# Moving operands laid at multiples of 64 bytes, block products reordered, and block sums made in place, in a two-layer diffusion trunk

## The chip, the cores and the metric

The kernel runs on one core of one Trainium2 chip. The metric is the device time of one execution in microseconds; the figure for a kernel is the median of its runs. A profile of one further execution gives the engines' instructions: PE (TensorE matmuls), PEld (its weight loads), DVE (VectorE), ACT (ScalarE), POOL (GpSimd) and SP (SyncE, which issues the DMAs).

## What is computed

Two layers over 1,024 latent tokens and 256 context tokens of width 1,024. Layer 0 mixes tokens by neighbourhood attention, layer 1 by sliding-window attention with grouped queries. Both end with a gated ConvFFN, which is where most of the change lies:

```python
def conv_ffn(h, w_up, conv_w, conv_b, w_down):
    t = h.shape[1]
    u = h @ w_up
    u_p = jnp.pad(u, ((0, 0), (CONV_W // 2, CONV_W // 2), (0, 0)))
    u = sum(u_p[:, tap:tap + t] * conv_w[tap] for tap in range(CONV_W)) + conv_b
    a, g = jnp.split(u, 2, axis=-1)
    return (a * jax.nn.silu(g)) @ w_down

for i in range(DEPTH):
    ...
    x = x + gt1 * (o @ w_out)
    ...
    h = modulate(rmsnorm(x, g_ffn[i]), sh2, sc2)
    x = x + gt2 * conv_ffn(h, ffn_w_up[i], ffn_conv_w[i], ffn_conv_b[i], ffn_w_down[i])
```

In layer 0 the context tokens go through the same ConvFFN; in layer 1 only the latents do.

## The kernel before

**Precision.** Every product is made of three: an operand is split into a high part (`hi`, a rounded copy made by ACT) and the rest (`lo`, the difference, made by DVE or POOL), and PE adds hi·hi, lo·hi and hi·lo into one bank. So one product step of the program is three matmuls: weights `whi`, `whi`, `wlo` against moving `hi`, `lo`, `hi`. In the FFN the weights are the stationary side, 128×128 at a time, and the activations the moving side: the moving operand is a row of 512 floats in each partition (256 for context tokens), of `b1hi`, `t12hi`, `t34h`, `b22hi` and their low parts, or of `ghi` and `glo` in the down projection.

**Up projection by blocks.** `ffn(l, ...)` runs the up projection of 1,024 tokens as a 2×2×2 block product with seven block multiplications instead of eight. The tokens are two halves (c = 0, 1), the 1,024 input features two halves (k below 4, and from 4), and the output pair of features (the `a` half and the `g` half of the gated product) the two column blocks. On the activation side this needs four sums of blocks, made once per layer: `t1` = X12−X11, `t2` = X22+shift−t1, `t3` = X22+dsh−X12, `t4` = X21+shift−t2 (X are the normalized and scaled tiles; `shift` and `dsh` bring in the adaLN shift). Each sum is then split into hi and lo: `t1`, `t2` in `t12hi`/`t12lo`, `t3`, `t4` in `t34h`/`t34l`. For each of the 22 feature tiles (`ft`) the weights need four sums too (`s`, from the two raw tiles `wraw`), and then seven products of 4 k-steps × 3 matmuls run on PE: 84 matmuls of 512 columns. `PROD` gives their order. The products go to four banks: `ua` (b11, then b21 on top), `ub` (t2), `uc` (t3, then t4), `ud` (t1, then b22). Between the two products of a bank ACT or DVE reads the bank's first state: ACT copies `ua` to the scratch `p1`, DVE adds `ub` to it, and so on, until the four quarters `c` of the tile's result are there. Then three convolution taps (`u`), SiLU, the product a·silu(g) on POOL, and a DMA of the tile to `g_dram`.

**Down projection.** `dn` reads `g_dram` back (`graw`), splits it into `ghi`, `glo`, splits the weights, and runs 22 × 8 × 3 matmuls of 512 columns for each token half of each layer: 2,112 in all. Each matmul reads `ghi` or `glo` as the moving operand.

**Context FFN.** In layer 0, `plan_ctx` runs the context's FFN (`uc`←`h2c`, 48 matmuls of 256 columns per feature tile, and `dnc`←`g`, 24) just ahead of the up projection; the block sums are made in its shadow. In layer 1 no context FFN stands there, so the normalization, the block sums and the first feature tile follow each other directly.

**Order of work.** A planner (`Sched`) is given operations with an engine, a duration, what they read and write, a key (a due time) and buffers to acquire and release; it plays them through and issues them in the order in which its model started them. On the chip each engine takes its own instructions strictly in that order, and waits on semaphores for the others. A change of keys or of dependencies therefore moves instructions on all engines. Since one wrapper issues every instruction, all of them carry line L79 in the profile, and one goes by tile names.

**Where tiles lie.** Tiles are allocated one behind another in a partition. In the built program of the kernel before, every tile starts at a multiple of 32 bytes. Of 16,148 matmuls, 4,712 have a moving operand that starts 32 bytes past a multiple of 64, the others start at a multiple of 64. The 4,712 are: all 2,112 of `dn` (512 columns), all 1,056 `uc`←`t34h`/`t34l` (512), all 528 of `dnc` (256), 592 `pv`←`pthi` and 304 `pv`←`ptlo` of attention (256), 96 `pv`←`pthi` (128) and 24 small ones of the norm. All other 512-column products of the FFN (`b1`, `t12`, `b22`) and of the output projection (`oacc`) start at a multiple of 64. The odd 32 bytes come from small tiles in front: `dsh`, 4 floats, in the FFN, and the attention scratch `S`, 644 floats, of which several buffers lie ahead of `pthi` and `ptlo`.

Of the kernel before, what the change touches and what calls it, by code (L numbers as in the profile page):

```python
# [241 lines left out]
def trunk_kernel(ctx, tc, xperm, xseq, cc, wmod, bmod, gnorm, na_wqkv, na_gq, na_gk, na_bias, na_wo,  # L242
# [334 lines left out]
    def plan_su(sc, key, I, units, groups, psa, wk, reads, write, n_add):  # L577
# [28 lines left out]
        for k in range(2):  # L606
# [98 lines left out]
    def plan_norm(sc, l, psa, wk, sums, x, hl, key):  # L705
# [46 lines left out]
        def dg(e):  # L752
            B["dg"] = wk.tile([P, 644], F32, tag="S", name="S", bufs=SBUFS)
# [11 lines left out]
        def bs(e):  # L765
            B["bc"] = wk.tile([P, 644], F32, tag="S", name="S", bufs=SBUFS)
# [472 lines left out]
    def ffn(l, opj, xt1, todo):  # L1239
# [117 lines left out]
        def plan_xload(c, key):  # L1357
            X[c] = Parts([None] * 4, 2)
            uses = 6 if c == 0 else 0
            for j in range(4):  # L1360
                def load(e, j=j):
# [4 lines left out]
                      acq=[("x", ("xt", c, j), uses or (4 if j < 2 else 8))])  # L1366
# [206 lines left out]
        sc.op("dve", 0.07, lambda e: dve.tensor_tensor(out=dsh, in0=shift[:, 4:8], in1=shift[:, 0:4], op=ALU.subtract),  # L1573
              writes=[("dsh",)], key=-50)
        rx = lambda c, k: [("xt", c, k // 2)] if X[c] is not xt1 or not last else []
        kb = 46.0 * n_todo
        for k in range(KT):
# [3 lines left out]
                      key + 0.5, rx(0, k))  # L1581
        for j in range(4):
            key = kb + (30.0 if not last else 2.0) * j
            for k in (j, j + 4):
                plan_t(1, 512, Nm[1], k, xap(1), xtok(1), scale, key)
            J = {}
            a, b = ("tr", j, "a"), ("tr", j, "b")
            x11, x21, x12, x22 = [lambda c=c, k=k: X[c][:, k, :] for c, k in ((0, j), (0, j + 4), (1, j), (1, j + 4))]
            k11, k21, k12, k22 = ("x", 0, j), ("x", 0, j + 4), ("x", 1, j), ("x", 1, j + 4)
            sh = shift[:, j + 4:j + 5]  # L1590
# [6 lines left out]
            def stt(out, in0, s, in1):  # L1597
                return lambda e: dve.scalar_tensor_tensor(out=out(), in0=in0(), scalar=s, in1=in1(), op0=ALU.add, op1=ALU.subtract)
            sc.op("dve", t_dve(512) + 0.06, stt(lambda J=J: J["a"][:, 512:], x22, sh, lambda J=J: J["a"][:, :512]),
                  reads=[k22, a + (1,)], writes=[a + (2,)], key=key, rel=rx(1, j + 4))  # L1600

            def t3(e, J=J, x12=x12, x22=x22, j=j):
                J["b"] = sr_tile("t34")
                dve.scalar_tensor_tensor(out=J["b"][:, :512], in0=x22(), scalar=dsh[:, j:j + 1], in1=x12(), op0=ALU.add,
                                         op1=ALU.subtract)
            sc.op("dve", t_dve(512) + 0.06, t3, reads=[k22, k12, ("dsh",)], writes=[b + (1,)], key=key, acq=[("sr", b, 2)],
                  rel=rx(1, j) + rx(1, j + 4))
            sc.op("dve", t_dve(512) + 0.06, stt(lambda J=J: J["b"][:, 512:], x21, sh, lambda J=J: J["a"][:, 512:]),
                  reads=[k21, a + (2,)], writes=[b + (2,)], key=key, rel=rx(0, j + 4))
            hcs = [("hc", k, "l") for k in range(KT)] if not last else []  # L1610
            for r, s, hi, lo, nm in ((a, "a", lambda j=j: t12h()[:, 2 * j:2 * j + 2, :].rearrange("p k t -> p (k t)"),
                                      lambda j=j: t12l(j).rearrange("p k t -> p (k t)"), "t12"),
                                     (b, "b", lambda j=j: t34_(0)[:, j, :], lambda j=j: t34_(1)[:, j, :], "t34")):
                sc.op("act", t_act(1024), lambda e, s=s, J=J, hi=hi: act.activation(hi(), J[s], AF.Copy), reads=[r + (1,), r + (2,)] + hcs,
                      writes=[(nm, j, "h")], key=key, rel=[r])
                sc.op(*LO[1024], lambda e, s=s, J=J, hi=hi, lo=lo: sub(e, lo(), J[s], hi().bitcast(F32)),
                      reads=[(nm, j, "h"), b + (2,)], writes=[(nm, j, "l")], key=key, rel=[r])

            hold = [("hcu",)] if not last else [("t34", i, "h") for i in range(4)] + [("b1", k, "l") for k in range(KT)]
            B22 = (512, j + 4, xap(1), xtok(1), shift, lambda j=j: b2h()[:, j, :], lambda j=j: b2l()[:, j, :], ("b2", j), key + 1,  # L1620
                   rx(1, j + 4))
            B["plan", j] = (hold, B22)
        for j in range(4):
            hold, a = B["plan", j]
            sc.op("x", 0.0, lambda e: None, reads=hold, writes=[("hcfree", j)], key=-100)
            n, k, x, xk, s, hi, lo, tok, key, rel = a
            sc.op("act", t_act(n), lambda e, hi=hi, x=x, k=k, s=s: act.activation(hi(), x(k), AF.Identity, bias=s[:, k:k + 1]),
                  reads=[xk(k), ("hcfree", j)], writes=[tok + ("h",)], key=key, rel=rel)
            sc.op("dve", t_dve(n) + 0.06, lambda e, hi=hi, lo=lo, x=x, k=k, s=s: dve.scalar_tensor_tensor(
                out=lo(), in0=x(k), scalar=s[:, k:k + 1], in1=hi().bitcast(F32), op0=ALU.add, op1=ALU.subtract),  # L1630
                reads=[xk(k), tok + ("h",)], writes=[tok + ("l",)], key=key, rel=rel)
# [7 lines left out]
            t1=(lambda j: (t12h()[:, 2 * j, :], t12l(j)[:, 0, :]), lambda j: ("t12", j)),  # L1639
            t2=(lambda j: (t12h()[:, 2 * j + 1, :], t12l(j)[:, 1, :]), lambda j: ("t12", j)),  # L1640
            t3=(lambda j: (t34_(0)[:, j, :512], t34_(1)[:, j, :512]), lambda j: ("t34", j)),
            t4=(lambda j: (t34_(0)[:, j, 512:], t34_(1)[:, j, 512:]), lambda j: ("t34", j)))
        PROD = (("a", 0, 0, "b11", True), ("b", 1, 0, "t2", True), ("a", 0, 512, "b21", False), ("c", 1, 512, "t3", True),
                ("d", 2, 0, "t1", True), ("c", 3, 0, "t4", False), ("d", 2, 512, "b22", False))

        def plan_up(ft):
            key = KU + 19.2 * ft
            pk = key - 24
            R, S, W = {}, {}, {}
            T = lambda *a: ("up", ft) + a  # L1650
# [15 lines left out]
            def plan_w(p, src, n, reads, rel, uses):  # L1666
                sc.op("act", t_act(n), whi(p, src, n), reads=reads, writes=[T("w", p, "h")], key=pk + p, acq=[("w", T("w", p), uses)],
                      rel=rel)
                sc.op(*LO[n], wlo(p, src, n), reads=reads + [T("w", p, "h")], writes=[T("w", p, "l")], key=pk + p, rel=rel)

            def s_op(e, t, c, make, a, b, op):
                if make:
# [5 lines left out]
                  reads=[rg] + ([("t34", 3, "h"), ("t34", 3, "l")] if ft else []),  # L1678
# [7 lines left out]
                  reads=[ra, T("s", 1), T("s", 2)], writes=[T("s", 4)], key=pk, rel=[ra])  # L1686
            plan_w(1, lambda: S[2], 1024, [T("s", 3), T("s", 4)], [T("s23")], 8)
            plan_w(2, lambda: S[1], 1024, [T("s", 4)], [T("s14")], 8)
# [4 lines left out]
            def plan_p(i):  # L1693
                d, p, col, b, first = PROD[i]
                ap, tok = BP[b]
                for j in range(4):
                    def mm(e, j=j):
# [4 lines left out]
                        for m, (w, x) in enumerate(((0, hi), (0, lo), (1, hi))):  # L1702
# [4 lines left out]
                          writes=[T("u", d)], key=key + 2.72 * i, acq=[("b", T("u", d), {"a": 2, "b": 1, "c": 2, "d": 2}[d])]  # L1707
                          if first and j == 0 else (), rel=[T("w", p)])
# [12 lines left out]
            sc.op("act", t_actp(512), p1, reads=[ua], writes=[st], key=key - 30, acq=[("sr", st, 3)], rel=[ua])  # L1721
# [5 lines left out]
            s_ = lambda: C["s"][:, :512]  # L1727
            tdp = t_dve(512) + 0.02
            sc.op("dve", tdp, pu(s_, "b", s_), reads=[ub], writes=[st], key=key - 30, rel=[ub])
# [565 lines left out]
```

## Time and profile before

| what | value |
|---|---|
| runs of the kernel | 3,006.07, 3,006.94, 3,008.57 us; median 3,006.94 |
| the profiled execution's own time | 3,010.63 us |
| its span from first to last instruction | 3,008.6 us |
| mean granted TensorE clock | 0.986 |
| matmuls in the profile | 16,608 |

The page gives busy time and instruction count of each engine, then the span in 40 slices with the busy share in tenths. A matmul's own duration in the profile overlaps the next one's, so what a matmul costs on a busy PE is the distance from its start to the start of the next; this text calls that the pitch. Starts are read from the timeline, whose rows are: start in us, duration in us, engine, line, operation, out<-in, shapes, count, and in brackets the idle time before it and what ended that.

### The profile page before, as it was taken

To read this page: it belongs to the slowest core of one execution; us is meant where nothing else is said; L and a number is where in the kernel's file an instruction comes from. 1 tells how busy PE (TensorE), PEld (TensorE's weight loads), DVE (VectorE), ACT (ScalarE), POOL (GpSimd) and SP (SyncE) were. 2 spreads that over 40 slices of the span, in tenths; PEclk is the share of its full clock that TensorE was granted. 3 is DMA by queue.
4 is the path that set the end of the run, shared out by engine and by line. 5 is a ranking of instruction groups with operands and counts; after the bars stand their busy time and mean duration, and the time that the engine had idled before them with its cause. 6 is when DMAs were issued, how large, how long until landed. Compare 5 with 4: busy or idle time off the path is not lost. (4 is left out here: it accounts for less than half of the span.)

```text
span 3008.6 us, 46247 instructions
## 1 busy us (share of the span) xinstructions
PE 2906.3 (97%) x16608; PEld 2509.3 (83%) x16608; DVE 2317.4 (77%) x4958; ACT 1638.7 (54%) x3168; POOL 740.4 (25%) x826
## 2 busy tenths in 40 slices
PE   6999999998999999999999999999998899999999
PEld 4999999998889977777788788988877688888887
DVE  7888888888787778787855659999987988887333
ACT  4777777777455534343433548887863444444222
POOL 2221222222110023232211025445421433332000
PEclk9999999999999999999999989999999999999999
DMA  6222222225645443434464630000133122224553
GB/s 234 61 84 81 84 83 62 75 76 157 215 156 188 154 164 122 144 123 137 141 224 147 219 122 29 14 31 14 68 125 118 69 79 77 85 84 168 170 170 102
DMA packets 126165, 349.88 MB, mean 116 GB/s; under 512 B 19440, under 2 KB 29168, under 8 KB 124528
## 3 DMA queue, kind: packets, MB, share of 16 engines
q1 hardware_dynamic: 125936, 346.94, 34.7%
q8 instruction: 131, 2.15, 0.3%
q14 instruction: 98, 0.80, 0.1%
HBM read 297.21 MB, written 49.68 MB: 115 GB/s over the span
## 5 line engine op out<-in xcount | busy, mean ns | idle before, releaser
L79 ACT ACTIVATE whi<-wraw 128x1024 fp32r<-128x1024 f32 (+1 forms) x264 | 240.9, 912 | 280.8 <-PE ua L79 160.5
L79 DVE TENSOR_TENSOR wlo<-wraw,whi 128x1024 fp32r<-128x1024 f32 (+1 forms) x216 | 242.8, 1125 | 71.5 <-ACT whi L79 70.4
L79 PE MATMUL dn<-ghi,whi 128*128 128x512 f32 x704 | 278.5, 396 | 0.6 <-ACT whi L79 0.6
L79 PE MATMUL dn<-glo,whi 128*128 128x512 f32 x704 | 278.2, 395 | 0.0
L79 PE MATMUL dn<-ghi,wlo 128*128 128x512 f32 x704 | 278.2, 395 | 0.0
L79 DVE TENSOR_TENSOR ptlo<-pt,pthi 128x512 fp32r<-128x512 f32 (+2 forms) x384 | 222.2, 595 | 37.9 <-ACT pthi L79 35.7
L79 DVE SCALAR_TENSOR_TENSOR u<-c,cv,u 128x1023 f32<-128x1023 f32 x176 | 246.7, 1420 | 0.1
L79 ACT ACTIVATE S<-S,m 128x640 f32<-128x640 f32 (+3 forms) x288 | 220.8, 768 | 39.1 <-DVE m L79 30.8
L79 POOL TENSOR_TENSOR wlo<-wraw,whi 128x512 fp32r<-128x512 f32 (+1 forms) x48 | 69.4, 1446 | 682.4 <-ACT whi L79 560.9
L79 ACT ACTIVATE whi<-s 128x1024 fp32r<-128x1024 f32 x88 | 93.3, 1062 | 263.5 <-PE uc L79 193.8
L79 DVE TENSOR_TENSOR glo<-graw,ghi 128x512 fp32r<-128x512 f32 x106 | 73.2, 692 | 212.4 <-ACT ghi L79 211.0
L79 ACT ACTIVATE pthi<-pt 128x512 fp32r<-128x512 f32 (+2 forms) x384 | 193.5, 524 | 55.8 <-PE pt L79 47.7
L79 ACT ACTIVATE ghi<-graw 128x512 fp32r<-128x512 f32 x110 | 69.1, 631 | 267.5 <-PE dn L79 247.4
L79 PE MATMUL pt<-idf,S 128*128 128x128 f32 x1280 | 198.3, 276 | 8.5 <-DVE S L79 3.8
L79 PE MATMUL mm<-whi,h0hi 128*128 128x384 f32 x512 | 181.1, 354 | 1.6 <-ACT qraw L79 1.6
L79 PE MATMUL mm<-wlo,h0hi 128*128 128x384 f32 x512 | 172.2, 336 | 0.0
L79 PEld LDWEIGHTS pt<-idf,S 128*128 128x128 f32 x1280 | 150.7, 141 | 20.6 <-DVE S L79 5.5
L79 PE MATMUL pv<-ptlo,v 128*128 128x256 f32 (+1 forms) x688 | 155.6, 300 | 6.5 <-DVE ptlo L79 6.0
L79 PEld LDWEIGHTS dn<-ghi,whi 128*128 128x128 f32 x704 | 132.0, 187 | 33.2 <-ACT whi L79 1.1
L79 POOL TENSOR_TENSOR qy<-qv,mhalf 128x4 f32<-128x4 f32 (+2 forms) x120 | 124.3, 1036 | 142.1 <-DVE qv L79 130.8
L79 PEld LDWEIGHTS dn<-ghi,wlo 128*128 128x128 f32 x704 | 132.0, 187 | 32.6 <-DVE wlo L79 0.4
L79 PEld LDWEIGHTS dn<-glo,whi 128*128 128x128 f32 x704 | 132.0, 187 | 32.5 <-DVE glo L79 0.5
(326 smaller groups left out, 9203.9 us busy)
## 6 DMA issues: line engine op xcount, KB each, us to landing
wraw<-in_w_up_dram SPq DMA_DIRECT2D x132, 512.0 KB, 3.5
wraw<-in_w_down_dram SPq DMA_DIRECT2D x88, 512.0 KB, 3.5
wm<-in_wmod_dram SPq DMA_DIRECT2D x80, 512.0 KB, 3.9
graw<-g_dram SPq DMA_DIRECT2D x110, 256.0 KB, 3.1
g_dram<-u SPq DMA_DIRECT2D x44, 512.0 KB, 2.6
slab<-in_na_wqkv_dram SPq DMA_DIRECT2D x32, 384.0 KB, 3.2
woraw<-in_na_wo_dram SPq DMA_DIRECT2D x24, 512.0 KB, 4.6
wraw<-in_w_down_dram SPq DMA_DIRECT2D x44, 256.0 KB, 3.2
```

The costliest lines, as they stand in the source:

```text
L79: r = f(*a, **k)
```

## The change

The diff, cut to its core (a line of "..." marks what is left out):

```diff
-                J["S", k] = wk.tile([P, 644], F32, tag="S", name="S", bufs=SBUFS)
+                J["S", k] = wk.tile([P, 656], F32, tag="S", name="S", bufs=SBUFS)
...
                 t34.extend(t34p.tile([P, 4, 1024], F32R, tag=f"t34{s}", name=f"t34{s}") for s in "hl")
+                t34p.tile([P, 8], F32, name="pad")
             return t34[i]
-        dsh = fp.tile([P, 4], F32, name="dsh")
+        dsh = fp.tile([P, 16], F32, name="dsh")
...
+        def parts(c, k, hi, lo, tok, key, rel, reads=()):
+            sc.op("act", t_act(512), lambda e: act.activation(hi(), X[c][:, k, :], AF.Copy), reads=[("x", c, k)] + list(reads),
+                  writes=[tok + ("h",)], key=key, rel=rel)
+            sc.op("dve", t_dve(512), lambda e: sub(e, lo(), X[c][:, k, :], hi().bitcast(F32)), reads=[("x", c, k), tok + ("h",)],
+                  writes=[tok + ("l",)], key=key, rel=rel)
+        def stt(c, k, c0, k0, s, c1, k1):
+            return lambda e: dve.scalar_tensor_tensor(out=X[c][:, k, :], in0=X[c0][:, k0, :], scalar=s, in1=X[c1][:, k1, :],
+                                                      op0=ALU.add, op1=ALU.subtract)
+        for step in range(3):
+            for j in range(4):
+                key = kb + (30.0 * j + 4 * step if not last else 2.0 * j + 8 * step)
+                if step == 0:
+                    plan_t(1, 512, Nm[1], j, xap(1), xtok(1), scale, key)
+                    sc.op("dve", t_dve(512), lambda e, j=j: dve.tensor_tensor(
+                        out=X[0][:, j, :], in0=X[1][:, j, :], in1=X[0][:, j, :], op=ALU.subtract), reads=[("x", 1, j)],
+                        writes=[("x", 0, j)], key=key)
+                    parts(0, j, ..., ("t1", j), key, ())
+                elif step == 1:
+                    plan_t(1, 512, Nm[1], j + 4, xap(1), xtok(1), scale, key)
+                    sc.op("dve", tst, stt(0, j, 1, j + 4, sh, 0, j), ...)
+                    parts(0, j, ..., ("t2", j), key, rx(0, j))
+                else:
+                    sc.op("dve", tst, stt(1, j, 1, j + 4, dsh[:, j:j + 1], 1, j), ...)
+                    parts(1, j, ..., ("t3", j), key, rx(1, j), hcs)
+                    sc.op("dve", tst, stt(0, j + 4, 0, j + 4, sh, 0, j), ...)
+                    parts(0, j + 4, ..., ("t4", j), key, rx(0, j + 4), hcs)
-            def t1(e, J=J, x11=x11, x12=x12):
-                J["a"] = sr_tile("t12")
-                ENG[e].tensor_tensor(out=J["a"][:, :512], in0=x12(), in1=x11(), op=ALU.subtract)
-            sc.op(*ADD, t1, reads=[k11, k12], writes=[a + (1,)], key=key, acq=[("sr", a, 2)], rel=rx(0, j) + rx(1, j))
...
-                sc.op("act", t_act(1024), lambda e, s=s, J=J, hi=hi: act.activation(hi(), J[s], AF.Copy), reads=[r + (1,), r + (2,)] + hcs,
-                      writes=[(nm, j, "h")], key=key, rel=[r])
...
-        PROD = (("a", 0, 0, "b11", True), ("b", 1, 0, "t2", True), ("a", 0, 512, "b21", False), ("c", 1, 512, "t3", True),
-                ("d", 2, 0, "t1", True), ("c", 3, 0, "t4", False), ("d", 2, 512, "b22", False))
+        PROD = (("a", 0, 0, "b11", True), ("d", 2, 0, "t1", True), ("b", 1, 0, "t2", True), ("a", 0, 512, "b21", False),
+                ("c", 1, 512, "t3", True), ("d", 2, 512, "b22", False), ("c", 3, 0, "t4", False))
...
+            WKEY = (-6, 2, 1, 14)
...
+                w = ("up0" if p == 0 else "up", ft, "w", p)
+                if p == 0 and ft > 1:
+                    reads = reads + [("up", ft - 2, "w", 1, "h")]
...
-                C["s"] = sr_tile("p1")
-                act.activation(C["s"][:, :512], U["a"], AF.Copy)
+                C["s"] = fp.tile([P, 512], F32, tag="glo", name="p1", bufs=GB)
+                act.activation(C["s"], U["a"], AF.Copy)
...
+            sc.op("dve", tdp, pu(s_, "d", lambda: c_tile("1")[:, 512:]), reads=[st, ud], writes=[T("c", 3)], key=key - 30,
+                  acq=[("x", T("ct", 1), 3)], rel=[("ud", ft), st])
...
-            sc.op("dve", tdp, pu(s_, "c", lambda: c_tile("1")[:, 512:]), reads=[st, uc], writes=[T("c", 3)], key=key - 30,
-                  acq=[("x", T("ct", 1), 3)], rel=[uc, st])
```

The padding gives every matmul of the program a moving operand that starts at a multiple of 64 bytes. The block sums are written over the `x` tiles that they are made from, on DVE alone, and split in halves of 512 columns instead of pairs of 1,024; before, `t1` could also go to POOL. `PROD` takes `t1` second and `t4` last, and the DVE and ACT reads of the banks follow. A bank's and a weight tile's turn is now kept apart by bank, so that the first two feature tiles' products can be mixed.

**PE at the start of layer 1's up projection.** `bc` is the matmul that spreads the norm over the partitions; the names `ua`, `ub`, `uc`, `ud` with one number belong to one feature tile. Before, behind the last `bc`:

```order
L79 MATMUL bc_27592<-nsum_27232,ones_89 128x128 x4
L79 MATMUL ub_27624<-t12hi_27612,whi_27432 128x512
L79 MATMUL ub_27624<-t12lo_27619,whi_27432 128x512
L79 MATMUL ub_27624<-t12hi_27612,wlo_27433 128x512
L79 MATMUL uc_27629<-t34h_27616,whi_27432 128x512
L79 MATMUL uc_27629<-t34l_27617,whi_27432 128x512
```

and with the change, from the 16th of the 18 matmuls of `ua_27574` on `b1` that stand behind the last `bc`:

```order
L79 MATMUL ua_27574<-b1hi_27306,whi_27556 128x512
L79 MATMUL ua_27574<-b1lo_27474,whi_27556 128x512
L79 MATMUL ua_27574<-b1hi_27306,wlo_27557 128x512
L79 MATMUL ud_27660<-t12hi_27641,whi_27434 128x512
L79 MATMUL ud_27660<-t12lo_27653,whi_27434 128x512
L79 MATMUL ud_27660<-t12hi_27641,wlo_27435 128x512
L79 MATMUL ud_27660<-t12hi_27641,whi_27434 128x512
L79 MATMUL ud_27660<-t12lo_27658,whi_27434 128x512
L79 MATMUL ud_27660<-t12hi_27641,wlo_27435 128x512
L79 MATMUL ud_27678<-t12hi_27641,whi_27665 128x512
L79 MATMUL ud_27678<-t12lo_27653,whi_27665 128x512
L79 MATMUL ud_27678<-t12hi_27641,wlo_27666 128x512
```

Before, the first product behind `bc` needs `t2`. Now 18 matmuls of the second feature tile on `b1` come first, and then 24 matmuls on `t1`, of two feature tiles (`ud_27660` and `ud_27678`).

**DVE at the same place.** `x_27163`, `x_27216` and so on are the pairs of normalized tiles of the second token half, `x_0` and `x_1` those of the first, `t` the separate tiles of the sums before. Before:

```order
L79 TENSOR_TENSOR wlo<-wraw,whi 128x1024
L79 SCALAR_TENSOR_TENSOR x_27163<-x_27163,modc,nsum 128x512
L79 SCALAR_TENSOR_TENSOR x_27216<-x_27216,modc,nsum 128x512
L79 TENSOR_TENSOR t_27606<-x_27163,x_0_26177 128x512
L79 SCALAR_TENSOR_TENSOR t_27608<-x_27216,dsh,x_27163 128x512
L79 SCALAR_TENSOR_TENSOR t_27606<-x_27216,modc,t_27606 128x512
L79 SCALAR_TENSOR_TENSOR x_27163<-x_27163,modc,nsum 128x512
L79 SCALAR_TENSOR_TENSOR t_27608<-x_1_26239,modc,t_27606 128x512
L79 SCALAR_TENSOR_TENSOR x_27216<-x_27216,modc,nsum 128x512
L79 TENSOR_TENSOR t12lo<-t_27606,t12hi 128x1024
L79 TENSOR_TENSOR t34l<-t_27608,t34h 128x1024
```

With the change:

```order
L79 TENSOR_TENSOR wlo<-wraw,whi 128x512
L79 SCALAR_TENSOR_TENSOR x_27172<-x_27172,modc,nsum 128x512 x2
L79 TENSOR_TENSOR x_0_26186<-x_27172,x_0_26186 128x512 x2
L79 SCALAR_TENSOR_TENSOR x_27194<-x_27194,modc,nsum 128x512
L79 TENSOR_TENSOR t12lo<-x_0_26186,t12hi 128x512 x2
L79 TENSOR_TENSOR x_0_26186<-x_27194,x_0_26186 128x512
L79 SCALAR_TENSOR_TENSOR x_27194<-x_27194,modc,nsum 128x512
L79 TENSOR_TENSOR wlo<-s,whi 128x1024
L79 TENSOR_TENSOR t12lo<-x_0_26186,t12hi 128x512
```

Before, all four sums of one k-step are made before the next k-step's. Now the four `t1` come first, then the four `t2`, then `t3` and `t4`; the split of a weight sum of the second feature tile (`wlo<-s`) stands among them.

**DVE in one feature tile later on.** Before, from the sum with `ub` on (`p` is the scratch, `c` the quarters, `u` the convolution):

```order
L79 TENSOR_TENSOR p_29543<-p_29543,ub 128x512
L79 TENSOR_TENSOR s<-wraw 128x512
L79 TENSOR_TENSOR s<-wraw,s 128x512
L79 TENSOR_TENSOR wlo<-wraw,whi 128x1024
L79 TENSOR_TENSOR c_29601<-p_29543,uc 128x512
L79 TENSOR_TENSOR wlo<-s,whi 128x1024
L79 TENSOR_TENSOR c_29601<-c_29601,ud 128x512
```

With the change:

```order
L79 TENSOR_TENSOR p_29561<-p_29561,ub 128x512
L79 TENSOR_TENSOR c_29597<-p_29561,ud 128x512
L79 TENSOR_TENSOR wlo<-wraw,whi 128x512
L79 TENSOR_TENSOR c_29597<-c_29597,uc 128x512
L79 TENSOR_TENSOR wlo<-s,whi 128x1024
L79 TENSOR_TENSOR s<-wraw 128x512
L79 TENSOR_TENSOR c_29616<-p_29561,ud 128x512
```

The sum that must be done before a bank is written again now waits for `uc` instead of `ud`, and the split of the half-width weights (`wlo`, 512 columns), before on POOL, stands ahead of it on DVE.

More of the change, by code (lines that the diff above doesn't have):

```diff
@@ L1623, in ffn @@
[L1623 to L1631, printed above, removed]
+                      key + 0.5)
@@ new lines, in ffn @@
+        hcs = [("hc", k, "l") for k in range(KT)] if not last else []
+        def parts(c, k, hi, lo, tok, key, rel, reads=()):
[3 more added lines that the diff above has]
+                  writes=[tok + ("l",)], key=key, rel=rel)
@@ new lines, in ffn @@
+        hold = [("hcu",)] if not last else [("t4", j, "l") for j in range(4)]
+        sc.op("x", 0.0, lambda e: None, reads=hold, writes=[("hcfree",)], key=-100)
+        for j in range(4):
+            key = kb + (30.0 * j + 12 if not last else 2.0 * j + 24)
+            k = j + 4
+            sc.op("act", t_act(512), lambda e, j=j, k=k: act.activation(b2h()[:, j, :], X[1][:, k, :], AF.Identity,
+                                                                        bias=shift[:, k:k + 1]),
+                  reads=[("x", 1, k), ("hcfree",)], writes=[("b2", j, "h")], key=key, rel=rx(1, k))
+            sc.op("dve", tst, lambda e, j=j, k=k: dve.scalar_tensor_tensor(
+                out=b2l()[:, j, :], in0=X[1][:, k, :], scalar=shift[:, k:k + 1], in1=b2h()[:, j, :].bitcast(F32), op0=ALU.add,
+                op1=ALU.subtract), reads=[("x", 1, k), ("b2", j, "h")], writes=[("b2", j, "l")], key=key, rel=rx(1, k))
@@ L1677, in plan_up @@
             sc.op(*ADD, lambda e: s_op(e, 1, 0, True, lambda: R["g"][:, :512], lambda: R["g"][:, 512:], ALU.add),
-                  reads=[rg] + ([("t34", 3, "h"), ("t34", 3, "l")] if ft else []),
+                  reads=[rg],
                   writes=[T("s", 1)], key=pk, acq=[("sr", T("s14"), 2)], rel=[rg])
```

95 lines of the change are left out of this document (38 added, 57 removed).

## The prediction

> **What bounds the kernel now.** I read the page's busy rows first, then the windows by stage, then the groups by shape, then the timeline of PE in the stages that the change touches.
>
> ```profile
> PE 2906.3 (97%) x16608; PEld 2509.3 (83%) x16608; DVE 2317.4 (77%) x4958; ACT 1638.7 (54%) x3168; POOL 740.4 (25%) x826
> ```
>
> PE is busy for 97% of the span, so only two things can pay: matmuls that follow each other faster, and the 3% in which PE waits. The windows (length, then busy time and count of PE, PEld, DVE, ACT, POOL, then granted clock, DMA share, GB/s) tell where each is:
>
> ```profile
> 850.00:910.00 60.00, 55.26 (x436) 53.71 (x435) 58.19 (x82) 37.47 (x53) 8.11 (x4) 0.97 0.46 150
> 1060.00:1465.00 405.00, 404.73 (x1979) 306.69 (x1980) 334.04 (x352) 156.32 (x171) 121.69 (x58) 1.00 0.42 138
> 1470.00:1755.00 285.00, 284.35 (x1243) 227.61 (x1242) 167.39 (x233) 121.95 (x187) 33.38 (x22) 1.00 0.58 191
> 2316.80:2346.00 29.20, 16.91 (x57) 11.64 (x55) 26.97 (x32) 12.30 (x15) 7.67 (x3) 0.82 0.00 1
> 2346.00:2370.00 24.00, 20.78 (x83) 16.18 (x82) 23.67 (x24) 10.80 (x12) 13.87 (x6) 0.93 0.25 86
> 2380.00:2760.00 380.00, 380.00 (x1661) 311.54 (x1660) 321.66 (x297) 164.10 (x181) 121.62 (x59) 1.00 0.25 88
> 2765.00:3000.00 235.00, 235.00 (x1009) 188.78 (x1008) 82.83 (x90) 63.17 (x80) 3.37 (x1) 1.00 0.46 154
> ```
>
> Up (1060 to 1465, 2380 to 2760) and down projection (1470 to 1755, 2765 to 3000) are PE end to end at the full clock; there only the pitch counts. The start of layer 1's up projection (2316.8 to 2370) is the one large hole: DVE is busy for 50.6 of 53.2 us, PE waits, and its clock falls to 0.82.
>
> **The pitch of aligned and offset operands.** The groups by shape give the first sign:
>
> ```profile
> L79 PE MATMUL dn<-ghi,whi 128*128 128x512 f32 x704 | 278.5, 396 | 0.6 <-ACT whi L79 0.6
> L79 PE MATMUL uc<-t34h,whi 128*128 128x512 f32 x352 | 143.2, 407 | 2.5 <-DVE c L79 2.5
> L79 PE MATMUL ua<-b1lo,whi 128*128 128x512 f32 x352 | 137.1, 389 | 0.0
> L79 PE MATMUL ud<-b22hi,whi 128*128 128x512 f32 x176 | 68.8, 391 | 0.0
> ```
>
> Same shape, yet the groups whose moving operand starts 32 bytes past a multiple of 64 (`dn`, `t34`) take longer than the aligned ones (`b1`, `b22`). The timeline of one steady feature tile shows it as pitch; each row is the first of 12 matmuls (the third and the fourth lie 36 apart):
>
> ```profile
> 2579.63 0.40 PE L79 MATMUL uc<-t34h,whi 128*128 128x512 f32 x1
> 2582.44 0.39 PE L79 MATMUL ud<-b22hi,whi 128*128 128x512 f32 x1
> 2585.17 0.39 PE L79 MATMUL ua<-b1hi,whi 128*128 128x512 f32 x1
> 2593.33 0.40 PE L79 MATMUL uc<-t34h,whi 128*128 128x512 f32 x1
> 2596.14 0.39 PE L79 MATMUL ud<-t12hi,whi 128*128 128x512 f32 x1
> 2598.87 0.40 PE L79 MATMUL uc<-t34h,whi 128*128 128x512 f32 x1
> ```
>
> Offset: 2.81 us for 12, both times, 234.2 ns each. Aligned: 2582.44 to 2593.33 is 48 matmuls in 10.89 us, 226.9 ns each. The same weights, clock and minute, so the difference is the operand. For the down projection the view of the tile `dn` from 2755 us on has count, durations, first and last start:
>
> ```profile
> L79 PE MATMUL dn<-ghi,whi x352: 393/396/399, 2758.3 to 3004.0; 128*128 128x512 f32 x176
> L79 PE MATMUL dn<-ghi,wlo x352: 393/396/397, 2758.8 to 3004.5; 128*128 128x512 f32 x176
> ```
>
> 1,056 matmuls (three such groups) start between 2758.3 and 3004.5: 246.2/1,055 = 233.4 ns. A row of 512 floats is 2,048 bytes; from a multiple of 64 it covers 32 blocks of 64 bytes, from 32 past it 33. One block more, at 226.9/32, is 7.1 ns, an estimate that fits both gaps (7.3 and 6.5).
>
> *Term A, down projection:* 2,112 × (233.4 − 226.9) = 13.7 us. *Term B, `uc` from `t34`:* 1,056 × (234.2 − 226.9) = 7.7 us. Both lie on PE in stages where nothing else waits, so all of it reaches the end: 21.4 us. Below, the bound is 0, if the tile and not its address makes the pitch. [...]
>
> The narrower products that were offset:
>
> ```profile
> 979.55 0.28 PE L79 MATMUL uc<-h2chi,whi 128*128 128x256 f32 x1
> 985.30 0.28 PE L79 MATMUL dnc<-ghi,whi 128*128 128x256 f32 x1
> 988.13 0.28 PE L79 MATMUL uc<-h2chi,whi 128*128 128x256 f32 x1
> ```
>
> 48 aligned in 5.75 us (119.8 ns), 24 offset in 2.83 us (117.9 ns): at 256 columns the offset costs nothing visible. *Term C*, 528 `dnc` and the 992 `pv` of attention: 0. At worst the aligned `dnc` come to 119.8, 1.0 us lost; at best all 1,520 gain 7.1 ns, 10.8 us. The row is nearest to 0.
>
> **The start of layer 1's up projection.** PE's rows with a wait (last figure: idle time, what ended it), and the `bc` behind which they begin:
>
> ```profile
> 2316.80 1.06 PE L79 MATMUL bc<-nsum,ones 128*128 128x128 f32 x8
> 2323.47 0.80 PE L79 MATMUL ub<-t12hi,whi 128*128 128x512 f32 x1 [5.62 <-ACT t12hi L79]
> 2325.50 0.80 PE L79 MATMUL ub<-t12lo,whi 128*128 128x512 f32 x1 [1.24 <-DVE t12lo L79]
> 2336.70 0.49 PE L79 MATMUL ub<-t12hi,whi 128*128 128x512 f32 x1 [2.46 <-ACT t12hi L79]
> 2338.73 0.69 PE L79 MATMUL ub<-t12lo,whi 128*128 128x512 f32 x1 [1.54 <-DVE t12lo L79]
> 2366.51 0.76 PE L79 MATMUL uc<-t34h,whi 128*128 128x512 f32 x1 [2.46 <-DVE c L79]
> ```
>
> At the full pitch, the 49 products and 8 `bc` up to 2346 need 49 × 0.227 + 1.06 = 12.2 of 29.2 us, the 83 after it 19.0 of 24.0: 22 us are lost, waits and half clock together. That is the ceiling of *term D*. The change reaches it only in part, since DVE's work stays. Its rows (and POOL's):
>
> ```profile
> 2318.99 1.41 DVE L79 SCALAR_TENSOR_TENSOR x<-x,modc,nsum 128x512 f32<-128x512 f32 x2
> 2320.32 0.68 DVE L79 TENSOR_TENSOR t<-x,x 128x512 f32<-128x512 f32 x1
> 2320.92 0.74 DVE L79 SCALAR_TENSOR_TENSOR t<-x,dsh,x 128x512 f32<-128x512 f32 x1
> 2325.37 1.22 DVE L79 TENSOR_TENSOR t34l<-t,t34h 128x1024 fp32r<-128x1024 f32 x1
> 2325.53 2.20 POOL L79 TENSOR_TENSOR t<-x,x 128x512 f32<-128x512 f32 x1 [10.25 <-DVE t12lo L79]
> 2326.50 1.77 DVE L79 SCALAR_TENSOR_TENSOR x<-x,modc,nsum 128x512 f32<-128x512 f32 x1
> 2344.19 1.23 DVE L79 TENSOR_TENSOR t34l<-t,t34h 128x1024 fp32r<-128x1024 f32 x1
> ```
>
> From start to start a scalar_tensor_tensor takes 0.665 us, a half-width sum 0.60, a full-width split 1.13. With the change DVE owes, from the first normalized tile to the last split of `t3`/`t4`, 20 of the first kind (13.3), 20 half-width sums and splits (12.0), one full-width weight split (1.1) and two sums from PSUM (1.2): 27.6 us, so 2318.99 + 27.6 = 2346.6. Before it was done at 2345.4. The three POOL sums that cost DVE 1.03 each (1.77 instead of 0.74) are gone, but four weight sums of the third feature tile now run on POOL in the same stretch, up to 4.1 us more. So DVE's last part comes 1.2 to 5.3 us later than before.
>
> PE, though, has more behind it by then. From the first `ua` on, before had issued 69 products at 2345.4; the order of the change has 96 ahead of that point (48 on `b1`, 24 on `t1`, 12 each on `t2` and `t3`). The lead is 27 × 0.227 = 6.1 us, less the 1.2 to 5.3: 0.8 to 4.9 us. Next late are the `b22` splits: behind the last `t4`, DVE adds `uc` (0.6), splits one `b22`, a weight and three more `b22` (4 × 0.665 + 1.13), 4.4 us, against 12 products (2.7 us) that PE can do meanwhile, so 1 to 2 us are lost again. After that nothing is missing: the waits at 2347 to 2366 (0.76 and 2.46) and the half clock that follows (0.07 of 24 us, 1.7 us) go, 4.9 in all. D = 2.8 (middle of 0.8 to 4.9) − 1.5 + 4.9 = 6.2 us, and I take 5.6 for the clock that the many short waits may still cost. The bounds: −3 us (the toll twice, no lead) and +22.
>
> **Where it is hidden.** In layer 0 the same sums lie beside the context FFN. The window 850 to 910 leaves DVE 1.8 of 60 us idle and PE 4.7, so an extra DVE instruction there shows on PE. The four `t1` go to DVE (4 × 0.60 = 2.4 us), but POOL's toll of up to 1.03 each goes with them: 0, ±3 us. In the steady tiles DVE takes a 0.60 split from POOL, 0.6 × 44 = 26 us of work, covered by waits like these:
>
> ```profile
> 2579.84 0.69 DVE L79 TENSOR_TENSOR c<-c,ud 128x512 f32<-128x512 f32 x1 [0.46 <-PE ud L79]
> 2582.64 0.69 DVE L79 TENSOR_TENSOR c<-p,uc 128x512 f32<-128x512 f32 x1 [2.12 <-PE uc L79]
> 2592.86 2.89 DVE L79 TENSOR_TENSOR s<-wraw,s 128x512 f32<-128x512 f32 x1
> ```
>
> DVE waits for PE 2.6 us in these two rows alone. Without that cover it would be 26 us on PE.
>
> **Sum.** 13.7 + 7.7 + 0 + 5.6 = 27.0 us. The profiled execution took 3,010.63 us, 2.0 more than its span and 3.7 more than the median of the runs; 3,010.6 − 27.0 = 2,983.6 for it, and 3,006.9 − 27.0 = 2,980 for the median.
>
> **Rivals.** *The start gains nothing* (12%): if POOL's toll is paid in full and the half clock returns, D is −3 to +2 and the time about 2,986. For it: DVE is the bound there before and after, and its work does not shrink. Against: the lead of 27 products is in the order.
>
> *The offset is not the cause* (9%): A and B vanish, D stays: 3,001. For it: 256-column products show no cost. Against: the two operand classes part at 512 columns without an overlap, in both stages.
>
> *The steady tile gets a new wait* (6%), the side of slower. `c`+=`uc` must now be done in the 12 products (2.72 us) between `t3` and `t4`, and the 0.60 split stands ahead of it on DVE. The row with 2.89 us is a DVE instruction that lay beside POOL's a·silu(g): if that falls on the sum, PE waits before `t4` in each of 44 tiles. From 27.0/44 = 0.61 us a tile on the kernel is slower than before; at 0.8 it is 2,980 + 35 = 3,015. Against: DVE waits for PE just there now, and the sum still comes first after PE's signal.
>
> *The start recovers almost all* (6%): if the toll is small and PE's clock stays up, D is 16 to 22 and the time about 2,967.
>
> **How the numbers follow.** The forecast has 67% and for itself 2,974 to 2,987 (D from −1 to +12). The range reaches down to 2,971 and up to 2,994, which leaves out the offset rival, the slow one and half of the last: 18%. A measurement here tells about 0.2%, 6 us, from no change: faster are the forecast, the first and the last rival and part of the second, 0.88; within 0.2%, the rest of the second and a small wait, 0.06; slower 0.06.
>
> **What would show it.** `dn` and `uc` at a pitch of 226 to 228 ns; `dnc` and `pv` unchanged; 18 `ua` behind `bc` without a wait, then many short waits for `t12lo` and `t34l` in place of 5.62 and 2.46 us; in the steady tile 84 matmuls in 19.05 us instead of 19.24. It is wrong if `dn` stays at 233, if a steady tile shows a wait `<-DVE c`, or if the stretch from `bc` to the third tile's first product is not shorter.

## The result, and the profile after

The changed kernel takes 3,018.09 us (median of 6 runs, 3,015.22 to 3,022.36) against 3,006.51 us before (6 runs). The ratio is 1.004, with a 95% interval of 1.0027 to 1.0053: it is slower by about 12 us, where 27 us faster was forecast. The profiled execution took 3,018.84 us, its span is 3,017.1.

The page's busy row, and then the windows of the stages (length, busy time and count of PE, PEld, DVE, ACT, POOL, granted clock, DMA share, GB/s):

```profile
PE 2899.7 (96%) x16608; PEld 2508.4 (83%) x16608; DVE 2288.1 (76%) x5014; ACT 1641.5 (54%) x3184; POOL 655.3 (22%) x786
```

```profile
850.00:910.00 60.00, 57.31 (x467) 56.90 (x467) 58.84 (x94) 38.78 (x60) 2.69 (x1) 0.97 0.48 158
1060.00:1465.00 405.00, 386.71 (x1866) 292.48 (x1859) 308.23 (x343) 148.29 (x163) 91.30 (x40) 0.99 0.39 126
2392.00:2770.00 378.00, 378.00 (x1654) 310.23 (x1653) 296.90 (x316) 163.23 (x181) 76.69 (x38) 1.00 0.25 88
2772.00:3012.00 240.00, 240.00 (x1050) 196.94 (x1049) 93.86 (x99) 67.75 (x85) 7.10 (x3) 1.00 0.47 159
```

PE is busy for less time in all than before (2,899.7 against 2,906.3 us), yet the span is longer: PE waits more. The second row says where. Layer 0's up projection, which had 404.73 of 405 us busy and 1,979 matmuls, now has 386.71 and 1,866. Layer 1's up projection is still full. Starts of PE's matmuls in the timeline give the length of each stage:

| from, to | before us | after us | difference |
|---|---|---|---|
| start to the first context product | 842.8 | 841.1 | −1.7 |
| context FFN and up projection of layer 0, to the first `dn` | 666.5 | 686.0 | +19.5 |
| down projection of layer 0 | 250.3 | 246.6 | −3.7 |
| attention of layer 1, to its FFN's last `bc` | 557.9 | 559.5 | +1.6 |
| start and up projection of layer 1, to the first `dn` | 440.8 | 437.6 | −3.2 |
| down projection of layer 1 | 246.2 | 241.5 | −4.7 |
| behind the last `dn` | 4.1 | 4.8 | +0.7 |

The sum is +8.5, the difference of the two spans. The view of PE's waits between 1060 and 1500 us has no row before, and one row now (us in total, times, longest):

```profile
PE mod L79 <- DMA wm<-in_wmod_dram: 21.9, 15, 3.4
```

`mod` is the product that works out layer 1's modulation; 48 of them, each with a load `wm` of 512 KB, are woven into layer 0's up projection. Layer 1 has none, and there nothing is lost.

The pitch moved less than forecast. The tile `dn` of layer 1 (count, durations, first and last start), and the first of 12 `uc`←`t34` with the first matmul behind them:

```profile
L79 PE MATMUL dn<-ghi,whi x352: 394/394/397, 2770.8 to 3011.8; 128*128 128x512 f32 x176
L79 PE MATMUL dn<-ghi,wlo x352: 392/392/397, 2771.3 to 3012.3; 128*128 128x512 f32 x176
```

```profile
2608.79 0.40 PE L79 MATMUL uc<-t34h,whi 128*128 128x512 f32 x1
2611.58 0.39 PE L79 MATMUL ud<-b22hi,whi 128*128 128x512 f32 x1
```

`dn` has (3,012.3 − 2,770.8)/1,055 = 228.9 ns instead of 233.4, and `uc` 2.79/12 = 232.5 instead of 234.2, though every moving operand now starts at a multiple of 64. So there are two questions: why PE waits for `wm`, and what sets the pitch.

**How the loads of `wm` became late.** `wm` and the raw weights `wraw` of the up projection share three buffers. In both kernels, SP's rows (loads are issued in this order) around two `mod` of one feature tile, with the instruction that gave the buffer back and the `mod` that needs the load. Before:

```profile
1174.17 1.30 POOL L79 TENSOR_TENSOR wlo<-wraw,whi 128x512 fp32r<-128x512 f32 x1 [11.46 <-ACT whi L79]
1175.49 5.23 SPq L79 DMA_DIRECT2D wm<-in_wmod_dram  x2
1179.69 0.64 PE L79 MATMUL mod<-wm,cpad 128*32 128x256 f32 x8
```

After:

```profile
1159.74 0.68 DVE L79 TENSOR_TENSOR s<-wraw,s 128x512 f32<-128x512 f32 x1
1160.34 0.68 DVE L79 TENSOR_TENSOR wlo<-wraw,whi 128x512 fp32r<-128x512 f32 x1
1160.50 1.05 SPq L79 DMA_DIRECT2D wm<-in_wmod_dram  x2
1163.02 0.39 PE L79 MATMUL ud<-b22hi,wlo 128*128 128x512 f32 x1
1165.02 0.64 PE L79 MATMUL mod<-wm,cpad 128*32 128x256 f32 x8 [1.61 <-DMA wm<-in_wmod_dram]
```

Before, POOL's split of the half-width weights was the last reader of its raw tile; its end (1,175.47) starts the load of `wm`, and PE comes to `mod` 4.2 us later, just when the load has landed (the two loads of this pair take 3.4 and 3.9 us). Now all three buffers are in use until DVE has made the last weight sum and that split, at 1,160.4 and 1,161.0; the load goes out then, and PE, which comes to `mod` 2.9 us after its issue, stands until 1,165.02. The SP rows of the view of waits (1060 to 1500 us) say the same, first before, then after:

```profile
SPq L79 <- POOL wlo L79: 182.3, 21, 10.4
```

```profile
SPq L79 <- DVE s L79: 110.1, 12, 14.1
SPq L79 <- DVE wlo L79: 54.1, 20, 9.5
```

### The profile page after: what moved, and what is told of

It is laid out like the page before. It is cut to its first block, busy times and chain, and to the rows that moved or that the text cites. A ratio compares the mean times of both kernels' runs of the same rounds, so it can differ in the third digit from the quotient of the medians.

```text
span 3017.1 us, 46240 instructions
## 1 busy us (share of the span) xinstructions
PE 2899.7 (96%) x16608; PEld 2508.4 (83%) x16608; DVE 2288.1 (76%) x5014; ACT 1641.5 (54%) x3184; POOL 655.3 (22%) x786
## 4 chain that ended last, share of the span: by engine, by line
PE 71%; DVE 17%; DMA 5%; ACT 3%; issue 3%; POOL 1%; SPq 0%; POOLq 0%; ACTq 0%; DVEq 0%
PE dn L79 15%; PE mm L79 13%; PE uc L79 11%; PE ud L79 6%; PE ua L79 5%; PE pt L79 5%; PE pv L79 4%; DVE S L79 3%; DMA wm<-in_wmod_dram 3%; PE oacc L79 3%; PE s L79 3%; PE ub L79 3%; PE dnc L79 2%; DVE ptlo L79 2%; DVE u L79 2%
## 5 line engine op out<-in xcount | busy, mean ns | idle before, releaser
L79 DVE TENSOR_TENSOR wlo<-wraw,whi 128x1024 fp32r<-128x1024 f32 (+1 forms) x259 | 278.9, 1077 | 98.5 <-ACT whi L79 97.3
L79 DVE SCALAR_TENSOR_TENSOR u<-c,cv,u 128x1023 f32<-128x1023 f32 x176 | 237.8, 1410 | 3.2 <-ACT u L79 3.2
L79 POOL TENSOR_TENSOR u<-u 128x1024 f32<-128x1024 f32 x42 | 105.0, 2500 | 401.9 <-DVE u L79 345.8
```

The costliest lines, as they stand in the source:

```text
L79: r = f(*a, **k)
```

## The experiments

**1. The last weight split earlier.** In the changed kernel:

```diff
-            WKEY = (-6, 2, 1, 14)
+            WKEY = (-6, 2, 1, 3)
```

> The changed kernel, with the key of the fourth weight split (the half-width one, from the raw tile of the gate half) set from 14 to 3, so that this raw buffer is given back earlier and the loads of wm stand ahead of the store of g in the load queue. Theory A (the changed kernel loses about 20 us in layer 0's up projection because the loads of wm get their raw buffer too late): the 13 waits of PE for wm of 0.6 to 3.5 us go, the stage is 15 to 20 us shorter, and the time is 2,996 to 3,004. Rival B (the loads themselves land late, since more traffic lies on the queue there): the waits stay and the time is 3,014 to 3,021.

Measured: 3,004.06 us (ratio to before 0.9993, 0.9983 to 1.0002), 14 us faster than the changed kernel; from the first `ua` to the first `dn` layer 0 takes 480.2 us instead of 493.5. The waits halve, but do not go:

```profile
PE mod L79 <- DMA wm<-in_wmod_dram: 12.4, 17, 1.1
```

Rival B is out by the time; a load of `wm` also takes hardly longer in the changed kernel (median 4.1 us from issue to landing, 3.9 before). Theory A holds in kind; its size was too high. The timeline shows what is left. DVE's split, the first pair of loads behind it, and the two `mod` that use them:

```profile
1147.57 1.78 DVE L79 TENSOR_TENSOR wlo<-wraw,whi 128x512 fp32r<-128x512 f32 x1
1149.38 4.84 SPq L79 DMA_DIRECT2D wm<-in_wmod_dram  x2
1153.20 0.64 PE L79 MATMUL mod<-wm,cpad 128*32 128x256 f32 x8 [1.03 <-DMA wm<-in_wmod_dram]
1158.07 0.64 PE L79 MATMUL mod<-wm,cpad 128*32 128x256 f32 x8
```

The first load of a pair still goes out only when that split ends (1,149.35), 2.8 us before PE comes to its `mod`, so PE waits; the second `mod` does not wait. Of the 17 waits 16 stand at the first `mod` of such a pair.

**2. The change in its two halves.** Only the paddings, in the order of before:

```diff
-                J["S", k] = wk.tile([P, 644], F32, tag="S", name="S", bufs=SBUFS)
+                J["S", k] = wk.tile([P, 656], F32, tag="S", name="S", bufs=SBUFS)
...
+                t34p.tile([P, 8], F32, name="pad")
...
-        dsh = fp.tile([P, 4], F32, name="dsh")
+        dsh = fp.tile([P, 16], F32, name="dsh")
```

> The kernel before with only the three paddings of the change (S, dsh, the pad behind t34); order of work as before. Theory of the prediction (offset of 32 bytes past a multiple of 64 costs 6.5 to 7.3 ns a matmul): dn and uc<-t34 at 226.7 ns, 21 us gained, 2,985. Theory from the trace of the changed kernel (64 bytes are not the whole of it): dn at 229 ns, uc<-t34 at 233 ns, 9 to 11 us gained, 2,996 to 2,998. If the paddings do nothing by themselves: 3,006.

Measured: 2,995.77 us (0.9964, 0.9949 to 0.9978): 10.2 us gained. `dn` runs at 228.9 ns again ((2,991.0 − 2,749.5)/1,055), and 12 `uc`←`t34` take 2.79 us. The theory of the prediction falls.

The other half is the changed kernel with the same lines undone:

> The changed kernel without the three paddings. If paddings and order add up: dn and uc<-t34 at 233 to 234 ns as before, and 9 to 11 us above the changed kernel, 3,027 to 3,029; PE waits for wm as in the changed kernel. If the waits for wm come from faster matmuls running ahead of the loads: they shrink, and the time is below 3,020.

Measured: 3,025.32 us (1.0069, 1.0054 to 1.0085), 7 us above the changed kernel and a little under the 3,027 to 3,029 of a plain sum. PE waits for `wm` at 13 of the same places, 18.1 us in all instead of 21.9. The paddings gain 10.2, the new order loses 19.4, and the two add up roughly; most of the waits do not come from faster matmuls.

**3. The new order without the loads of `wm`.** In both kernels the 48 products and their loads are left out:

```diff
-            for n in range(48):
+            for n in range(0):
                 plan_mod(sc, 1, n // KT, ...)
```

> The kernel before without the 48 loads of wm and their products in layer 0's up projection (layer 1's modulation is a constant instead, so its numbers differ). Both theories: about 48 x 0.47 us = 23 us of PE less, 2,980 to 2,985.

> The changed kernel without the same 48 loads and products. Theory A (the loss is PE's wait for wm and nothing else in the new order): the waits go with the loads, and it is 8 to 14 us faster than nomod_before, 2,968 to 2,975. Rival H (the new order loses in layer 0's up projection by itself, the wait for wm is only where it shows): it is 5 to 12 us slower than nomod_before, 2,986 to 2,996.

Measured: 2,966.22 and 2,947.56 us, so the new order with its paddings is 18.7 us faster here, more than theory A had said. The up projection of `nomod_after` is full:

```profile
1060.00:1440.00 380.00, 380.00 (x1663) 311.86 (x1663) 299.63 (x319) 161.25 (x178) 77.51 (x39) 1.00 0.23 83
```

Rival H is out: the loss is the wait for `wm`, and without it the order is worth 18.7 − 10.2 = 8.5 us, if the paddings gain as much here as they did with the loads. Leaving the loads out saved 39 us before, not 23: a feature tile falls from 20.8 to 21.8 us to 19.24, with two or three `mod` in it.

**4. The pitch by itself.** A kernel of nothing but matmul chains:

> Leaves out the whole computation: only chains of 48 matmuls of 512 columns, three for each step as in the kernel (hi, lo, hi), with the moving operand at chosen places of one tile, the other engines idle, and at the end the same with VectorE and ScalarE busy. Theory of the prediction: 226.7 ns at 0 and 64 past a multiple of 128 bytes, 233.4 at 32 and 96, wherever it lies. Theory C (the place decides: before, every offset operand also lay above 180 KB of the partition and every aligned one of 512 columns below 90 KB): 226.7 at 24 and 64 KB whatever the offset, 229 to 234 from 136 KB on. Theory D (128 bytes count): above 136 KB 229 at 0 and 233 at 32, 64 and 96. Theory E (contention with other engines): 226.7 everywhere while they are idle, more only in the last part.

The pitch is (start of the 48th − start of the 4th)/44 of a chain; at 0 it is 226.7 once a chain is settled, and over a whole chain 226.7 at 24 KB and 227.2 at the other places; what makes these 0.5 ns was not tried:

| start of the moving operand past a multiple of 128, weights at 0 | 24 KB | 64 KB | 136 KB | 180 KB | 196 KB | 180 KB, once more |
|---|---|---|---|---|---|---|
| 0 | 226.7 | 227.2 | 227.2 | 227.2 | 227.2 | 227.2 |
| 32 | 233.3 | 233.4 | 233.3 | 233.3 | 233.3 | 233.3 |
| 64 | 228.8 | 228.8 | 228.8 | 228.8 | 228.9 | 228.8 |
| 96 | 233.6 | 233.6 | 233.6 | 233.6 | 233.6 | 233.6 |

The copies that were to keep VectorE and ScalarE busy beside the last chains did not run there. The page's slices (15.4 us each) show them at the start:

```profile
DVE  9994000000000000000000000000000000000000
ACT  9999910000000000000000000000000000000000
```

So the last column only repeats the fourth. The chains at 24 KB, from 38 to 81 us, are the ones with company: ScalarE is busy beside all four, VectorE beside the first and part of the second, and they give what the others give, to 0.5 ns. Neither the region nor these two engines count here (C and D fall, and E for these two), and 32 bytes cost as the prediction said (233.3 against 226.7 ns). But 64 is not 0: the 228.8 of the changed kernel's `dn` is here, at 64 past a multiple of 128, while `dn` stood at 0. In that kernel the weights `whi` and `wlo` start at 64 past a multiple of 256, here at 0. So the next run tried the difference of the two starts:

> Leaves out the whole computation: chains of 48 matmuls as in the run before, now with the moving operand at every 32 bytes over 512, and with the weights also 32 and 64 bytes past a multiple of 512; then 384 and 256 columns. Theory F (what counts is the start of the moving operand less the start of the weights, over 512 bytes): at a difference of 0 and 512 226.7 ns wherever the weights start, 228.8 at 64, 233 at 32, and at 384 and 416, the differences of uc<-t34 in the changed kernel and before, 233. Theory G (the start of the moving operand alone counts, over 128 bytes): 226.7 to 227.2 at each multiple of 128 with the weights at any place, 228.8 at 64 past it; uc<-t34 would then be explained by nothing that this run has.

| moving start less weight start, over 256 bytes | 0 | 32 | 64 | 96 | 128 | 160 | 192 | 224 |
|---|---|---|---|---|---|---|---|---|
| pitch at 512 columns, ns | 226.7 | 233.3 | 228.8 | 233.6 | 233.3 | 234.2 | 233.3 | 233.3 |

From 256 on the values repeat (226.7, 233.3, 228.8, 233.6, 233.3, ...). With the weights moved by 64, a moving start at 64 gives 226.7 and at 128 gives 228.9; with the weights moved by 32, a start at 32 gives 227.4 over the chain (226.7 once it is settled) and at 0 gives 233.3. Theory F holds, with 256 in place of 512; G falls. The difference does not fix the last nanosecond: at 128 over 256 two more chains, at other places, gave 232.2 and 232.3 instead of 233.3. The rule explains each pitch of the kernels to that measure:

| operand | difference over 256 | the chain says | measured in the kernel |
|---|---|---|---|
| `b1`, `t12`, `b22` before | 0 | 226.7 | 226.9 |
| `dn` before | 32 | 233.3 | 233.4 |
| `uc`←`t34` before | 160 | 234.2 | 234.2 |
| `dn` after | 64 | 228.8 | 228.9 |
| `uc`←`t34` after | 128 | 233.3 | 232.5 |

**5. The operands put where the difference is 0**, in the order of before:

```diff
-    invd = cpool.tile([P, 1], F32, name="invd")
+    invt = cpool.tile([P, 8], F32, name="invd")
+    invd = invt[:, 0:1]
...
+                t34p.tile([P, 104], F32, name="pad")
...
-        dsh = fp.tile([P, 4], F32, name="dsh")
+        dsh = invt[:, 4:8]
```

> The kernel before, order of work unchanged, but the four numbers of dsh put into a free corner of the tile of invd, and t34 behind a pad of 416 bytes, so that ghi, glo, t34h and t34l all start 64 bytes past a multiple of 512, as b1, t12, b22 and the weights whi, wlo do. Theory F: dn and uc<-t34 at 226.7 ns, 3,168 x 6.6 ns = 21 us gained, 2,983 to 2,987. Theory G: the operands stand at the 64 of theory G, dn at 228.8 and uc<-t34 at 233, 2,996.

Measured: 2,987.85 us (0.9943, 0.9928 to 0.9957), 17.4 us faster than before. Both operands are at the full pitch; `dn` has 239.1/1,055 = 226.6 ns, `uc` 2.72/12 = 226.7:

```profile
L79 PE MATMUL dn<-ghi,whi x352: 389/389/389, 2747.2 to 2985.8; 128*128 128x512 f32 x176
L79 PE MATMUL dn<-ghi,wlo x352: 388/389/389, 2747.6 to 2986.3; 128*128 128x512 f32 x176
```

```profile
2603.00 0.39 PE L79 MATMUL uc<-t34h,whi 128*128 128x512 f32 x1
2605.72 0.39 PE L79 MATMUL ud<-t12hi,whi 128*128 128x512 f32 x1
```

Each matmul now lasts 389 ns, as those of `ua`←`b1lo` did before. The median is a little above the 2,983 to 2,987 expected. By stages, the down projections gain 6.2 and 7.1 us and layer 1's up projection 3.9. Layer 0's context and up projection, where 528 × 7.5 ns = 4.0 were due, is 1.0 longer than before: 528 `dnc` cost 2 ns more each (1.1 us), PE waits once for `wm` (2.1 us), and the rest is not explained.

**6. Both mends in the changed kernel.** The places of 5 in the order of the change:

> The changed kernel with the places of rel0 (dsh in the corner of invd, 416 bytes behind t34), nothing else. Theory F: dn from 229 to 226.7 and uc<-t34 from 233 to 226.7 ns, 2,112 x 2.2 + 1,056 x 6 = 11 us, of which the 3 us of layer 0's up projection may be eaten by the waits for wm, which stay: 3,007 to 3,010.

Measured: 3,009.56 us (1.0009, 0.9999 to 1.0018), as expected: better places alone do not help the waits. Then a buffer of its own for `wm`, taken from the scratch `sr`, which no longer holds the block sums; the planner, which counts 1.8 us for such a load, is told 4.2:

```diff
+        SRB = 4 if last else 3
...
-            st["raw"] = rpool.tile([P, 1024], F32, tag="raw", name="wm")
+            st["raw"] = raw() if raw else rpool.tile([P, 1024], F32, tag="raw", name="wm")
...
-        sc.op("dma", 1.8, load, ..., acq=[("raw", I + ("raw",), 1)])
+        sc.op("dma", lat, load, ..., acq=[("wm" if raw else "raw", I + ("raw",), 1)])
...
+                         raw=lambda: fp.tile([P, 1024], F32, tag="wm", name="wm", bufs=1), lat=4.2)
```

> The same, and in layer 0's ConvFFN the loads of wm get a buffer of their own in place of one of the four tiles of the scratch sr; the planner is told 4.2 us for a load of wm there instead of 1.8. Theory A: the waits for wm go, and with the places of rel0 it is faster than rel0 by what the new order gained without the loads (nomod_after against nomod_before 18.7, less the 10.2 that the paddings gave alone: 8.5 us), 2,977 to 2,982. Rival: three tiles of sr are too few for the weight sums and the context, new waits come, 2,985 to 2,996.

Measured: 2,985.18 us (0.9925, 0.9909 to 0.9942). No wait for `wm` is left, and the window that had 386.71 us busy is full:

```profile
1060.00:1465.00 405.00, 405.00 (x1988) 309.56 (x1989) 305.88 (x373) 159.10 (x175) 85.34 (x42) 1.00 0.41 135
```

Yet it missed 2,977 to 2,982 and lies in the rival's range. Three tiles of `sr` are too few, as the rival said, but not for the weight sums: layer 0's down projection became 4.3 us longer than that of rel0 (248.4 against 244.1). Its tiles read back from `g_dram` use `sr` too:

```diff
-                    J["g"] = sr_tile("graw")
+                    J["g"] = fp.tile([P, 1024], F32, tag="wm", name="graw", bufs=1) if own else sr_tile("graw")
```

with `own` true for each fourth tile of layer 0.

> own_wm, and in layer 0's down projection each fourth tile read back from g goes into the buffer of wm, which is free by then, so that four such tiles are in flight again. If the 4.3 us that layer 0's down projection of own_wm was longer than that of rel0 (248.4 against 244.1) come from the fourth tile that it lacked: 2,980 to 2,983. If they come from the work that the new order leaves to its first microseconds: 2,984 to 2,987, with the same waits for ghi and glo.

Measured: 2,978.68 us (0.9913, 0.9896 to 0.9929), a little better than expected; that down projection takes 245.0 us, so the fourth tile was 3.4 of the 4.3. It is 9.2 us faster than rel0, close to the 8.5 of experiment 3, and the fastest kernel of the study: 26 us under the kernel before of its runs (3,005.04), 39 under the change.

## Why the prediction was wrong, point by point

**The side was wrong, for one step that it did not take.** "Where it is hidden" costed the half-width weight split as 0.60 us of DVE time per tile, covered by DVE's waits, and so put at nothing in the sum. That held in layer 1: its tiles take 19.21 us instead of 19.24 with no new wait. But the split is also the instruction that gives back a raw weight buffer, and `wm` loads into it. The prediction followed the moved instructions on PE, DVE and POOL, and not what each of them releases, nor SP's queue behind that. The waits for `wm` cost 21.9 us in the view of waits, and without these loads the order gains (experiment 3). The rival on the side of slower had the size (3,015) and the wrong mechanism: it looked for a wait on `c` in all 44 tiles, and there are 15 on `wm` in layer 0 alone.

**Terms A and B were mis-sized, since the rule behind them was half right.** "One block of 64 bytes more" fitted 6.5 and 7.3 ns. The runs show another rule: the difference of moving and weight start over 256 bytes (in the chains 226.7 ns at 0, 228.8 at 64, 233.3 at 32, 234.2 at 160). The trace of before could not tell them apart: all aligned operands of 512 columns had the difference 0, all offset ones 32 or 160. The paddings moved `dn` to 64 and `t34` to 128, so A gave 3.7 + 4.7 = 8.4 us instead of 13.7, and B, by the two pitches, 1,056 × (234.2 − 232.5) = 1.8 instead of 7.7. Experiment 5 gets 17.4 of the 21.4 us.

**Term C was right where it could be read.** `dnc` stayed at 118 ns. Attention is 1.6 us longer, but over all the runs that stage took 553.8 to 559.5 us, with aligned and with offset `pv` mixed, so nothing is shown.

**Term D was 2.6 us instead of 5.6**, by the 3.2 of the stage less 19 tiles × 0.03. The signs forecast are there: 18 `ua` behind `bc` without the old wait, then several waits in place of 5.62 and 2.46 us, one of them still 3.3. In the view of PE's waits from 2333 to 2392 us the longest are:

```profile
PE ud L79 <- DVE t12lo L79: 3.7, 2, 3.3
PE uc L79 <- ACT t34h L79: 3.1, 3, 1.8
PE uc L79 <- DVE t34l L79: 1.3, 3, 0.6
```

What went against it is POOL's toll on DVE. The prediction left it between nothing and 4.1 us, and so had DVE's last part 1.2 to 5.3 us later. DVE finishes `t34l` 32.1 us after its first normalized tile (2,334.25 to 2,366.3), against 26.4 before: 5.7 later, above the upper end, so almost nothing of the lead of 6.1 us is left. The order of DVE's work is the one that was counted. Four of its instructions, one under each of POOL's four weight sums, take some 1.05 us more each, 4.2 in all; the rows show three of them, at 1.7 us instead of 0.6 to 0.7:

```profile
2343.31 3.45 DVE L79 SCALAR_TENSOR_TENSOR x<-x,modc,nsum 128x512 f32<-128x512 f32 x2
2346.68 1.74 DVE L79 TENSOR_TENSOR t12lo<-x,t12hi 128x512 fp32r<-128x512 f32 x1
```

```profile
2342.31 2.22 POOL L79 TENSOR_TENSOR s<-s,wraw 128x512 f32<-128x512 f32 x1 [4.29 <-issue]
2344.49 1.71 POOL L79 TENSOR_TENSOR s<-wraw 128x512 f32<-128x512 f32 x1
2346.17 1.71 POOL L79 TENSOR_TENSOR s<-wraw,s 128x512 f32<-128x512 f32 x1
```

PE's clock fell there again (0.85 from 2333 to 2390).

**The layer-0 context stage was forecast at 0 ± 3 and gains.** In the pair without `wm`, the stretch from the first context product to the first `dn` is 625.7 before and 619.4 after: 6.3 us. Starts of `ua` place them. Ahead of the first `ua` the stretch is 0.6 us shorter, though 24 `dnc` (2.8 us) stand there that stood in the first feature tile before; that tile is 4.8 shorter, 2.8 of them by this move; the tiles behind it give 0.9, which is the pitch of `t34` (528 × 1.7 ns). So 3.4 us belong to the context and 2.0 to the first tile. What causes them was not tried; in the kernels with `wm`, from 850 to 910 us PE is busy for 57.31 us instead of 55.26, with one instruction of POOL there instead of four.

## What to carry to other kernels

When an instruction moves, ask what it releases, and which load waits in the queue for that buffer; the slack here was 0.3 us (4.2 from release to use, 3.9 in the median for the load), and it was lost when 4.2 became 2.9. Before an alignment is given as the cause of a pitch, list all addresses that the slow and the fast class differ in, the other operand's too; a chain of 48 matmuls for each place settles it for 11 us of device time. Here, at 512 columns, give the moving operand a start that differs from that of the weights by a multiple of 256 bytes: 226.7 ns in the chains, against 228.8 to 234.2 at the other differences.

## What was not expected of the hardware

- The pitch of a 512-column float32r matmul with a weight load before each hangs in the chains on the distance between moving and weight start, with a period of 256 bytes: 226.7 ns at 0, 228.8 at 64, 232.2 to 234.2 at the other multiples of 32 tried with all operands alike. What causes it was not shown; the runs show the relation only. The place of the weights counts too: a moving start at 64 gives 228.8 ns with the weights at 0 and 226.7 with the weights at 64.
- At 256 columns the order in the chains is another: 120.0 ns at a distance of 0, 117.8 at 32 and 64, 113.4 at 192. At 384 columns 0, 64 and 256 give 173.3 and 128 and 384 give 176.1. In experiment 5, with `ghi` put to distance 0, `dnc` went from 118 up to 120 ns.
- One of three operands out of place can cost more than all three: in the chains, with `hi` at 0 and `lo` at 64, the mean is 231.9 ns, with both at 64 it is 228.8.
- A group of `mod` (8 small matmuls on one `wm`) with what hangs on it costs some 0.8 us in a full stage (39 us saved by leaving out 48), not the 0.47 that had been reckoned from their own starts.
